# A hybrid decoder block: the first MLP group by plain products with a down product of its own, block sums built behind it, and down products that start with the last 256 tokens

## The chip, the cores and the metric

The kernel runs on one core of a Trainium2 chip. Five engines work side by side, each through its own instructions in order: PE (TensorE, matmuls), DVE (VectorE), ACT (ScalarE), POOL (GpSimd) and SP (SyncE, here the queue that issues nearly all loads). They wait for each other only where one needs what another has made. The metric is the device time of one execution in microseconds (us), and the time of a kernel is the median of its runs.

## The reference, cut to what matters

The block mixes 16 + 512 tokens (a delta-net branch and a sparse attention branch, merged and projected) and then applies an MLP with squared ReLU. The change touches the MLP alone; `h` has 512 rows that count and 1024 columns, `w_up` is 1024 x 4096 and `w_down` 4096 x 1024.

```
h = h + _rmsnorm(mix, post_mix_norm)
n2 = _rmsnorm(h, pre_mlp_norm)
u = jnp.square(jax.nn.relu(jnp.einsum('btd,df->btf', n2, w_up)))
h = h + _rmsnorm(jnp.einsum('btf,fd->btd', u, w_down), post_mlp_norm)
```

## The kernel before, in words

Every float32 operand of a matmul is split into a rounded part `hi` (ACT copies it) and a rest `lo` (DVE subtracts), and a product is three matmuls: hi x hi, hi x lo, lo x hi. The norm in front of the MLP is not applied to its operand: the row factor is taken out (squared ReLU is homogeneous), `mlp_scale` computes it, and only `down_last` uses it.

**Operands of the MLP.** The transposed tokens form a 2 x 2 matrix of blocks: rows are the two halves of the 1024 columns of `h`, columns the first 256 tokens (token tiles 0 and 1) and the second 256 (tiles 2 and 3). They are B11, B21 (first tokens), B12, B22 (second tokens). `mix_more(t)` transposes token tile t on PE (`n2t`), scales it into `fblock` (tile `F`) and lets `operand` make hi and lo.

**Up products.** `w_up` is taken in 8 groups of 512 columns; a group's weights are a 2 x 2 matrix of blocks too (A11, A12, A21, A22, each 128 x 1024 as laid out). `up(g)` multiplies the two matrices by Winograd's form of Strassen's scheme: seven products instead of eight, each of 24 matmuls of 128x256 (`product`). The scheme needs sums of blocks: of the weights (S1 to S4, in the tile `Ssum`, made per group by DVE) and of the tokens (T1 to T4, made once). `hidden(g, i, j, ..)` adds what belongs together, applies the squared ReLU and writes hi and lo of `u` for column half i and token half j.

**Down products.** `down(gs)` multiplies `u` of one or two groups by `w_down`: for each half of the 1024 output columns four PSUM tiles `d`, one for each token tile, gather over the chunks of weights (`proj_half`, whose matmuls are the lines 502 to 504 of `rows_part`), and `evac` copies (first time) or adds (later) them into `macc`. `down_last` does it for the last group.

**The order.** Groups 0 and 1 start interleaved, since only B11 and B21 exist while token tiles 2 and 3 are still being finished: the products A11 x B11 and A12 x B21 of both groups first (matmuls into X and Z of each), then the token sums T1 to T4, then the five others of group 0, of group 1, then `down((0, 1))` with four chunks for each half. From group 2 on it is `up(g)`, `down((g,))`, seven products and 96 matmuls of 128x512. The weights of groups 2 to 7 are loaded into the tile `R`, which lies in the slot `s6` and so wait until `u` of group 1, which lies there, has been used by its down product. A scheduler places instructions of the program on each engine by priority, so neighbouring steps mix.

Names in the rows: `d302` is `d` of group 3, column half 0, token tile 2. Views without such numbers write `d`. `hi_d`, `lo_d`, `side_pair` and `lo_side` hold weights; `raw_d` and `raw_up` are loads before they are split.

Of the kernel before, what the change touches and what calls it, by code (L numbers as in the profile page):

```python
# [10 lines left out]
F32 = mybir.dt.float32  # L11
# [3 lines left out]
ALU = mybir.AluOpType  # L15
# [23 lines left out]
def hybrid_block(ctx: ExitStack, tc: tile.TileContext, io: dict):  # L39
# [463 lines left out]
                TE.matmul(pt, lh, wlo, start=False, stop=False)  # L503
                TE.matmul(pt, ll, whi, start=False, stop=end)  # L504

    def proj_half(src, name, lhs, evac, chunks=4, room=lambda: None):

        pts = [stile(f"{name}{t}") for t in range(4)]
        for c in range(chunks):
            w = wload(src[c], 1024, f"{name}{c}", room())  # L510
            for t in range(NT):
                rows_part(pts[t], [(c, w)], lhs, t, slice(0, 512), c == 0, c == chunks - 1)
        for t in range(NT):
            evac(pts[t], t)

    def proj_rows(src, name, lhs, evac, done, more, room):
# [530 lines left out]


    bop = {x: mp.tile([P, 2, 4, 256], F32R, name=f"bop{x}") for x in ("B11", "B21", "B22", "T1")}
    late = {}  # L1050
    F = [cst.tile([P, 1024], F32, tag="st", name=f"F0{x}", bufs=2) for x in range(2)] + [wk.tile([P, 1024], F32, tag="tb", name=f"F1{x}", bufs=2) for x in range(2)]

    def fblock(b, t):

        return F[2 * b + t // 2][:, 512 * (t % 2) : 512 * (t % 2) + 512].rearrange("p (k t) -> p k t", t=P)

    def operand(x, t, src):
        nonlocal last_n2
        o = (bop[x] if x in bop else late[x])[:, :, :, t % 2 * P : t % 2 * P + P]
        S.copy(o[:, 0], src)  # L1060
        last_n2 = V.tensor_tensor(o[:, 1], src, f(o[:, 0]), ALU.subtract)

    def mix_more(t):

        for b in range(2):
            ps = stile(f"n2t{t}{b}")
            for k in range(4):
                kk = 4 * b + k
                TE.transpose(ps[:, k * P : (k + 1) * P], h2[:, t, kk * P : (kk + 1) * P], ident)
            gm = gmT[:, 4 * b : 4 * b + 4].rearrange("p (k o) -> p k o", o=1).to_broadcast([P, 4, P])  # L1070
            V.tensor_tensor(fblock(b, t), ps.rearrange("p (k t) -> p k t", t=P), gm, ALU.mult)
            if t < 2 or b:
                operand(f"B{b + 1}{t // 2 + 1}", t, fblock(b, t))
        if t > 1:
            b11, b21, b12, b22 = (fblock(b, u) for u in (t - 2, t) for b in range(2))
            V.tensor_tensor(b11, b12, b11, ALU.subtract)
            operand("T1", t, b11)
            V.tensor_tensor(b12, b22, b12, ALU.subtract)
            V.tensor_tensor(b22, b22, b11, ALU.subtract)
            V.tensor_tensor(b21, b21, b22, ALU.subtract)  # L1080

    def late_operands():
        t23 = slots.tile([P, 2, 2, 4, 256], F32R, tag="s1", name="t23")
        late["T2"], late["T3"] = t23[:, 0], t23[:, 1]
        for t in (2, 3):
            operand("T2", t, fblock(1, t))
        for t in (2, 3):
            operand("T3", t, fblock(0, t))
        t4 = [cst.tile([P, 1024], F32R, tag="st", name=f"t4{x}", bufs=2) for x in range(2)]
        for t in (0, 1):  # L1090
            o = [x.rearrange("p (k t) -> p k t", t=256)[:, :, t * P : t * P + P] for x in t4]
            S.copy(o[0], fblock(1, t))
            V.tensor_tensor(o[1], fblock(1, t), f(o[0]), ALU.subtract)
        late["T4"] = t4

    def mlp_scale(t):
        s1 = wk.tile([P, 1], F32, tag="s1", name=f"s1{t}", bufs=2)
        S.activation(gx[:, 1, :], h2[:, t, :], AF.Square, accum_out=s1)
        rms(rmlp[:, t : t + 1], s1, t, 1.0 / D, f"n2{t}")
        V.tensor_tensor(rmlp[:, t : t + 1], rmlp[:, t : t + 1], rmlp[:, t : t + 1], ALU.mult)  # L1100
        V.tensor_scalar(rmd[:, t : t + 1], rmlp[:, t : t + 1], rmlp[:, t : t + 1], 1.0 / D, ALU.mult, ALU.mult)

    def o_evac(pt, t, c0, n, i):
        cs = slice(c0, c0 + n)
# [23 lines left out]
    def pair(name):  # L1128

        nonlocal turn  # L1130
        turn += 1
        x = turn % (4 if "pair" in side else 3)
        if x == 3:
            return side["pair"]
        hi = wp.tile([P, 1024], F32R, tag="hl", name=f"hi_{name}", bufs=5)
        return [hi, side["lo"] if x == 2 else wp.tile([P, 1024], F32R, tag="hl", name=f"lo_{name}", bufs=5)]

    def up_block(i, k, g):

# [23 lines left out]
    def hidden(g, i, j, a, b=None):  # L1163
# [8 lines left out]
        o = us[g][:, :, 2 * i : 2 * i + 2, 256 * j : 256 * j + 256]  # L1172
        split(o[:, 0], o[:, 1], u.rearrange("p (a t) -> p a t", t=256))

    def up(g):

        first = g < 2
        nm = f"up{g}"
        if first:
            early = quarters_of(slots.tile([P, 4, 1024], F32R, tag="s2", name="eroom")) if g == 0 else None  # L1180
            rooms = [early[0:2], early[2:4]] if g == 0 else [[wp.tile([P, 1024], F32R, tag="hl", name=f"hl{g}{i}{x}", bufs=5) for x in range(2)] for i in range(2)]
            ws = []
            for k in range(2):
                raw = wp.tile([P, 1024], F32, tag="raw", name=f"raw_{nm}{k}", bufs=2)
                load(raw, 0, k, g)
                ws.append(parts(raw, rooms[k]))
            Z = ptile(f"{nm}Z")
            X = ptile(f"{nm}X", sp if g else pp)
            yield
            product(X, ws[0], bop["B11"], True)  # L1190
            E1 = copied(X, "cb", f"E1{g}")
            product(Z, ws[1], bop["B21"], True)
            yield
            us[g] = slots.tile([P, 2, 4, L], F32R, tag=("s2", "s6")[g], name=f"u{g}")
            hidden(g, 0, 0, E1, Z)
            yield
            R = {"21": gx[:, 2, :], "22": gx[:, 3, :]}
            for x in ("11", "12"):
                R[x] = wp.tile([P, 1024], F32, tag="raw", name=f"raw_{nm}{x}", bufs=2)
        else:  # L1200
            R = {x: side["R"][:, i, :] for i, x in enumerate(("11", "12", "21", "22"))}
        if "S" not in side:
            side["S"] = wk.tile([P, 1024], F32, tag="tb", name="Ssum", bufs=2)
            side["lo"] = wk.tile([P, 1024], F32R, tag="tb", name="lo_side", bufs=2)
        s_ = side["S"]
        for x in ("11", "21", "22", "12") if not first else ("21", "22", "11", "12"):
            load(R[x], int(x[0]) - 1, int(x[1]) - 1, g)
        if not first:
            X = ptile(f"{nm}X")
            product(X, parts(R["11"], pair(f"{nm}A11")), bop["B11"], True)  # L1210
            E1 = copied(X, "cb", f"E1{g}")
            us[g] = slots.tile([P, 2, 4, L], F32R, tag="s2", name=f"u{g}")
        V.tensor_tensor(s_, R["21"], R["22"], ALU.add)
        Y = ptile(f"{nm}Y")
        product(Y, parts(s_, pair(f"{nm}S1")), bop["T1"], True)
        E5 = copied(Y, "ca", f"E5{g}")
        V.tensor_tensor(s_, s_, R["11"], ALU.subtract)
        product(X, parts(s_, pair(f"{nm}S2")), late["T2"], False)
        U = copied(X, "cv", f"U{g}")
        V.tensor_tensor(s_, R["12"], s_, ALU.subtract)  # L1220
        product(Y, parts(s_, pair(f"{nm}S4")), bop["B22"], False)
        hidden(g, 0, 1, U, Y)
        V.tensor_tensor(R["21"], R["11"], R["21"], ALU.subtract)
        product(X, parts(R["21"], pair(f"{nm}S3")), late["T3"], False)
        hidden(g, 1, 1, E5, X)
        if not first:
            Z = ptile(f"{nm}Z")
            product(Z, parts(R["12"], pair(f"{nm}A12")), bop["B21"], True)
            hidden(g, 0, 0, E1, Z)
        product(X, parts(R["22"], pair(f"{nm}A22")), late["T4"], False)  # L1230
        hidden(g, 1, 0, X)

    def lhs(gs):
# [4 lines left out]
    def down(gs):  # L1238
# [9 lines left out]
        for hf in range(2):  # L1248
            c0 = 2 * (gs[0] % 2)
            n = 2 * len(gs)  # L1250
            proj_half(io["w_down"][g // 2][hf][c0 : c0 + n], f"d{g}{hf}", lhs(gs), lambda pt, t: evac(pt, t, hf), n, lambda: pair("d"))

    def down_last(g):

# [28 lines left out]
                d_evac(pt, t, cuts[i], n, i, end and i == 2)  # L1283
            out(t, len(cuts) - 1)

    ups = [up(g) for g in range(2)]
    for _ in range(3):
        for u in ups:
            next(u)
    late_operands()  # L1290
    with tc.issue_after(last_n2.ins):
        for t in range(NT):
            mlp_scale(t)
    for u in ups:
        for _ in u:
            pass
    down((0, 1))
    side["pair"] = quarters_of(slots.tile([P, 4, 1024], F32R, tag="s5", name="side_pair"))[0:2]
    turn = 3
    side["R"] = slots.tile([P, 4, 1024], F32, tag="s6", name="R")  # L1300
    for g in range(2, NG):
        for _ in up(g):
            pass
        if g < NG - 1:
            down((g,))
        else:
            down_last(g)
# [68 lines left out]
```

## Time and profile before

| | |
|---|---|
| median of 3 runs | 1092.55 us (1090.36 to 1095.31) |
| the profiled execution | 1095.43 us |
| its span in the profile | 1093.5 us |
| PE, DVE, ACT busy | 95%, 72%, 44% of the span |
| mean granted clock of PE | 0.978 of full speed |

The span runs from the first to the last instruction; 1.9 us of the execution lie around it. The granted clock is 1.00 at 2.4 GHz and 0.50 at 1.2 GHz, so a row between them mixes both. Starts are microseconds from the beginning of the span. The MLP of this profile runs from about 691 us to the end.

### The profile page before, as it was taken

The page shows a single profiled execution, that of the slowest core. Times are in us where ns is not written, and L with a number is a line of the kernel's source. Part 1 is how long each engine was busy: PE and PEld are TensorE (multiplying, and loading weights), DVE is VectorE, ACT ScalarE, POOL GpSimd, SP SyncE. Part 2 cuts the span into 40 slices and gives each one's busy share as a digit, 9 for nine tenths or more (in the row PEclk, how much of TensorE's full clock was granted, in tenths as well). Part 3 has the DMA queues.
Part 4 walks back from the last instruction along what each step waited for, and adds up shares of the span by engine and source line. Part 5 has one row for each costly group of instructions (what it writes and reads, how often), then busy time and mean ns, then how long its engine had stood idle before and what let it go on. Part 6 is the DMA issues. An engine that isn't in the chain of part 4 may idle for free.

```text
span 1093.5 us, 16951 instructions
## 1 busy us (share of the span) xinstructions
PE 1034.0 (95%) x6717; PEld 919.9 (84%) x6717; DVE 784.4 (72%) x1596; ACT 482.4 (44%) x852; POOL 62.2 (6%) x85
## 2 busy tenths in 40 slices
PE   7999999999999999999999999869978999999995
PEld 6999999989987888988888888768867978889794
DVE  5797898427599999668775546997146667576677
ACT  5555565444367522347655223454233324233241
POOL 4202303000000000000000000000000000000003
PEclk9999999999999999999999999989988999999997
DMA  5433425110132222231112363222333223133112
GB/s 174 124 110 88 127 79 147 44 39 21 59 100 76 70 86 97 97 97 58 59 39 78 97 221 107 77 78 97 97 116 116 82 92 117 59 115 97 58 39 78
DMA packets 33424, 98.61 MB, mean 90 GB/s; under 512 B 3696, under 2 KB 4032, under 8 KB 33344
## 3 DMA queue, kind: packets, MB, share of 16 engines
q1 hardware_dynamic: 30624, 89.60, 25.8%
q0 software_dynamic: 2720, 7.92, 3.1%
q8 instruction: 53, 0.87, 0.3%
q14 instruction: 27, 0.22, 0.1%
HBM read 92.23 MB, written 5.28 MB: 89 GB/s over the span
## 4 chain that ended last, share of the span: by engine, by line
PE 78%; DVE 13%; DMA 3%; ACT 3%; issue 2%; SPq 0%; DVEq 0%; ACTq 0%
PE d L502 5%; PE d L503 5%; PE d L504 5%; PE pa_dense L886 2%; PE pa_dense L885 2%; PE pa_dense L884 2%; PE pb_z L543 1%; PE pa_q L192 1%; PE pa_q L194 1%; PE pa_bg L192 1%; PE pa_q L193 1%; PE pa_bg L193 1%; PE bd L1006 1%; PE bd L1007 1%; PE bd L1005 1%
## 5 line engine op out<-in xcount | busy, mean ns | idle before, releaser
L502 PE MATMUL d<-hi_d,u 128*128 128x512 f32 (+1 forms) x212 | 84.1, 397 | 5.5 <-ACT u L700 5.5
L504 PE MATMUL d<-hi_d,u 128*128 128x512 f32 (+1 forms) x212 | 82.9, 393 | 0.0
L503 PE MATMUL d<-lo_d,u 128*128 128x512 f32 (+1 forms) x140 | 54.9, 392 | 0.0
L502 PEld LDWEIGHTS d<-hi_d,u 128*128 128x128 f32 x212 | 40.3, 190 | 15.1 <-ACT u L700 6.1
L504 PEld LDWEIGHTS d<-hi_d,u 128*128 128x128 f32 x212 | 40.1, 189 | 9.4
L884 PE MATMUL pa_dense<-nhi,hi_dense 128*128 128x512 f32 x96 | 39.3, 409 | 0.0
L97 ACT CAST hi_d<-raw_d 128x1024 fp32r<-128x1024 f32 x26 | 27.3, 1050 | 25.3 <-PE d L503 12.7
L886 PE MATMUL pa_dense<-nhi,lo_dense 128*128 128x512 f32 x96 | 38.1, 397 | 0.0
L885 PE MATMUL pa_dense<-nlo,hi_dense 128*128 128x512 f32 x96 | 38.0, 396 | 0.0
L543 PE MATMUL pb_z<-hi_z,nhi 128*128 128x256 f32 x128 | 37.6, 294 | 0.0
L192 PE MATMUL pa_k<-nhi,hi_k 128*128 128x264 f32 x128 | 37.1, 290 | 0.0
L192 PE MATMUL pa_v<-nhi,hi_v 128*128 128x264 f32 x128 | 37.0, 289 | 0.0
L192 PE MATMUL pa_q<-nhi,hi_q 128*128 128x258 f32 x128 | 36.8, 287 | 0.0
L194 PE MATMUL pa_k<-nhi,lo_k 128*128 128x264 f32 x128 | 36.7, 288 | 0.0
L544 PE MATMUL pb_z<-lo_z,nhi 128*128 128x256 f32 x128 | 36.6, 286 | 0.0
L545 PE MATMUL pb_z<-hi_z,nlo 128*128 128x256 f32 x128 | 36.4, 285 | 0.0
L194 PE MATMUL pa_v<-nhi,lo_v 128*128 128x264 f32 x128 | 36.4, 284 | 0.0
L193 PE MATMUL pa_v<-nlo,hi_v 128*128 128x264 f32 x128 | 36.4, 284 | 0.0
L193 PE MATMUL pa_k<-nlo,hi_k 128*128 128x264 f32 x128 | 36.3, 284 | 0.0
L194 PE MATMUL pa_q<-nhi,lo_q 128*128 128x258 f32 x128 | 36.1, 282 | 0.0
L193 PE MATMUL pa_q<-nlo,hi_q 128*128 128x258 f32 x128 | 36.0, 281 | 0.0
L700 ACT CAST u<-u 128x512 fp32r<-128x512 f32 x32 | 19.7, 619 | 28.1 <-DVE u L1171 22.5
(875 smaller groups left out, 3459.5 us busy)
## 6 DMA issues: line engine op xcount, KB each, us to landing
raw_d<-w_down SPq DMA_DIRECT2D x32, 512.0 KB, 3.6
R<-w_up SPq DMA_DIRECT2D x24, 512.0 KB, 3.9
raw_k<-w_k SPq DMA_DIRECT2D x8, 512.0 KB, 4.0
raw_v<-w_v SPq DMA_DIRECT2D x8, 512.0 KB, 4.5
raw_q<-w_q SPq DMA_DIRECT2D x8, 512.0 KB, 3.5
raw_z<-w_z SPq DMA_DIRECT2D x8, 512.0 KB, 3.7
raw_w_ga<-w_ga SPq DMA_DIRECT2D x8, 512.0 KB, 3.6
raw_bg<-w_bg SPq DMA_DIRECT2D x8, 512.0 KB, 3.6
```

What stands on the lines that cost most here:

```text
L192: TE.matmul(pt[:m, :n], hi[:, ws], mh[:, k, ms], start=(k == 0), stop=False)
L193: TE.matmul(pt[:m, :n], hi[:, ws], ml[:, k, ms], start=False, stop=False)
L194: mark = TE.matmul(pt[:m, :n], lo[:, ws], mh[:, k, ms], start=False, stop=(k == KT - 1))
L502: TE.matmul(pt, lh, whi, start=beg, stop=False)
L503: TE.matmul(pt, lh, wlo, start=False, stop=False)
L504: TE.matmul(pt, ll, whi, start=False, stop=end)
L543: TE.matmul(pt, nhi[:, k, ts], whi, start=(k == 0), stop=False)
L544: TE.matmul(pt, nhi[:, k, ts], wlo, start=False, stop=False)
L545: mm = TE.matmul(pt, nlo[:, k, ts], whi, start=False, stop=(k == KT - 1))
L884: TE.matmul(pt, hi[:, ws], nhi[:, k, NM:], start=(k == 0), stop=False)
L885: TE.matmul(pt, hi[:, ws], nlo[:, k, NM:], start=False, stop=False)
L886: mm = TE.matmul(pt, lo[:, ws], nhi[:, k, NM:], start=False, stop=(k == KT - 1))
```

## The change

It replaces the interleaved start of groups 0 and 1. Group 0 is now done by `up_plain`: eight plain products (192 matmuls of 128x256, in four PSUM tiles of 48), whose operands are B11, B21, B12, B22 and weights without sums. Then come the token sums, `down((0,))` alone, `mlp_scale` for all four token tiles at once, `up(1)` by the seven products, `down((1,))`, and the rest as before. B12 is a new operand; T3 later takes its place in the same tile. `u` of group 0 lies in slot `s6`, that of group 1 in `s2`. Every `down` now takes the token tiles in the order 2, 3, 0, 1.

```
-    def proj_half(src, name, lhs, evac, chunks=4, room=lambda: None):
+    def proj_half(src, name, lhs, evac, chunks=4, room=lambda: None, order=range(NT)):
...
-            for t in range(NT):
+            for t in order:
                 rows_part(pts[t], [(c, w)], lhs, t, slice(0, 512), c == 0, c == chunks - 1)
-        for t in range(NT):
+        for t in order:
             evac(pts[t], t)
...
-            if t < 2 or b:
-                operand(f"B{b + 1}{t // 2 + 1}", t, fblock(b, t))
-        if t > 1:
+            operand(f"B{b + 1}{t // 2 + 1}", t, fblock(b, t))
+
+    def token_sums():
+        for t in (2, 3):
             b11, b21, b12, b22 = (fblock(b, u) for u in (t - 2, t) for b in range(2))
             V.tensor_tensor(b11, b12, b11, ALU.subtract)
             operand("T1", t, b11)
...
+    def mlp_scale():
+        sm = wk.tile([P, NT], F32, tag="s1", name="s1n", bufs=2)
+        for t in range(NT):
+            S.activation(gx[:, 1, :], h2[:, t, :], AF.Square, accum_out=sm[:, t : t + 1])
+        V.tensor_scalar(sm, sm, 1.0 / D, EPS, ALU.mult, ALU.add)
+        rsqrt(rmlp, sm, (P, NT), "n2")
...
+    def up_plain(g):
+
+        early = quarters_of(slots.tile([P, 4, 1024], F32R, tag="s2", name="eroom"))
+        ws = [wload(io["w_up"][4 * g + m], 1024, f"up{g}{m}", (early[0:2], early[2:4], None, None)[m]) for m in range(4)]
+        us[g] = slots.tile([P, 2, 4, L], F32R, tag="s6", name=f"u{g}")
+        for j in range(2):
+            for i in range(2):
+                pt = ptile(f"up{g}{i}{j}")
+                for m in range(2):
+                    hi, lo = ws[2 * i + m]
+                    o = pt[:, 256 * m : 256 * m + 256]
+                    for k in range(KT):
+                        b = bop[f"B{k // 4 + 1}{j + 1}"]
+                        ks = slice(k * P, (k + 1) * P)
+                        for n, (x, y) in enumerate(((hi, 0), (hi, 1), (lo, 0))):
+                            TE.matmul(o, x[:, ks], b[:, y, k % 4, :], start=m + k + n == 0, stop=m == 1 and k == KT - 1 and n == 2, skip_group_check=True)
+                hidden(g, i, j, pt)
...
-            proj_half(io["w_down"][g // 2][hf][c0 : c0 + n], f"d{g}{hf}", lhs(gs), lambda pt, t: evac(pt, t, hf), n, lambda: pair("d"))
+            proj_half(io["w_down"][g // 2][hf][c0 : c0 + n], f"d{g}{hf}", lhs(gs), lambda pt, t: evac(pt, t, hf), n, lambda: pair("d"), (2, 3, 0, 1))
...
-    ups = [up(g) for g in range(2)]
...
-    down((0, 1))
+    up_plain(0)
+    token_sums()
+    down((0,))
+    mlp_scale()
+    up(1)
+    down((1,))
```

The first place is PE's order behind the transposes of token tile 3 (`n2t30`, `n2t31`). Before, one product of group 1 follows, and then the first product that needs a weight sum and T1 (`up0Y`):

```order
L1069 MATMUL n2t30_7129<-ident_78,h2_6714 128x128 x4
L1069 MATMUL n2t31_7135<-ident_78,h2_6714 128x128 x4
L1156 MATMUL up1X_7180<-bopB11_6724,hl100_7167 128x256 x2
L1156 MATMUL up1X_7180<-bopB11_6724,hl101_7168 128x256
L1156 MATMUL up0Y_7389<-bopT1_6727,hi_up0S1_7390 128x256 x2
L1156 MATMUL up0Y_7389<-bopT1_6727,lo_up0S1_7391 128x256
```

Now the second tokens' plain products follow (B12 is the first half of the tile `b12t2`), 96 matmuls in two PSUM tiles, and then the down product of group 0:

```order
L1072 MATMUL n2t30_7126<-ident_78,h2_6714 128x128 x4
L1072 MATMUL n2t31_7134<-ident_78,h2_6714 128x128 x4
L1191 MATMUL up001_7279<-b12t2_7115,eroom_7149 128x256
L1191 MATMUL up011_7333<-b12t2_7115,hi_up02_7160 128x256
L1191 MATMUL up001_7279<-b12t2_7115,eroom_7149 128x256 x11
L1191 MATMUL up001_7279<-bopB22_6726,eroom_7149 128x256 x12
L1191 MATMUL up011_7333<-b12t2_7115,hi_up02_7160 128x256
L1191 MATMUL up011_7333<-b12t2_7115,lo_up02_7161 128x256
L502 MATMUL d002_7415<-hi_d_7417,u0_7170 128x512
L503 MATMUL d002_7415<-lo_d_7418,u0_7170 128x512
```

Between the transposes and the first matmul on a block sum there were 24 matmuls; there are now 96 of them and the 96 matmuls of a down product.

The second place is SP's queue ahead of group 2. Before, the loads of group 2's weights (`R`) stand behind all loads of the double down product:

```order
L93 DMA raw_d112_7910<-w_down 128x1024
L93 DMA raw_d113_7940<-w_down 128x1024
L93 DMA raw_d200_8208<-w_down 128x1024
L93 DMA raw_d201_8238<-w_down 128x1024
L1143 DMA R_7973<-w_up 128x2x512 x8
L93 DMA raw_d210_8276<-w_down 128x1024
```

Now they stand behind the first load of group 1's down product, ahead of its three others:

```order
L1144 DMA raw_up111_7572<-w_up 128x2x512
L1144 DMA raw_up112_7573<-w_up 128x2x512
L93 DMA raw_d100_7813<-w_down 128x1024
L1144 DMA R_7943<-w_up 128x2x512 x4
L93 DMA raw_d101_7843<-w_down 128x1024
L93 DMA raw_d110_7880<-w_down 128x1024
```

What they wait for is the slot `s6`: it was the end of `down((0, 1))` and is now the end of `down((0,))`.

The third place is PE's first down matmuls of group 3 (groups 4 to 6 read alike). Before:

```order
L1156 MATMUL up3X_8341<-t40_7302,lo_up3A22_8534 128x256
L502 MATMUL d300_8566<-hi_d_8570,u3_8370 128x512
L503 MATMUL d300_8566<-lo_side_7383,u3_8370 128x512
L502 MATMUL d301_8567<-hi_d_8570,u3_8370 128x512
L503 MATMUL d301_8567<-lo_side_7383,u3_8370 128x512
L502 MATMUL d302_8568<-hi_d_8570,u3_8370 128x512
```

Now:

```order
L1157 MATMUL up3X_8311<-t40_7407,lo_up3A22_8504 128x256
L502 MATMUL d302_8538<-hi_d_8540,u3_8340 128x512
L503 MATMUL d302_8538<-lo_side_7575,u3_8340 128x512
L504 MATMUL d302_8538<-hi_d_8540,u3_8340 128x512
L502 MATMUL d303_8539<-hi_d_8540,u3_8340 128x512
L503 MATMUL d303_8539<-lo_side_7575,u3_8340 128x512
L502 MATMUL d300_8536<-hi_d_8540,u3_8340 128x512
```

Twelve matmuls on token tiles 2 and 3 now stand ahead of the first on tile 0.

## Rows read from the trace of the kernel before

**Rows 1.** The page's busy shares.

```profile
PE 1034.0 (95%) x6717; PEld 919.9 (84%) x6717; DVE 784.4 (72%) x1596; ACT 482.4 (44%) x852; POOL 62.2 (6%) x85
```

**Rows 2.** What PE waited for from 690 us to the end: us in total, times, longest (eleven rows, 33.9 us together; the five smallest, 2.7 us, are left out).

```profile
PE d L502 <- ACT u L700: 10.6, 5, 3.3
PE up0Y L1156 <- ACT hi_up0S L700: 9.1, 1, 9.1
PE up2X L1156 <- ACT hi_up2A L700: 5.1, 1, 5.1
PE up1Y L1156 <- DVE lo_up1S L701: 2.6, 1, 2.6
PE up1Z L1156 <- DVE hl L701: 2.1, 1, 2.1
PE n2t L1069 <- DVE h L1042: 1.7, 2, 1.4
...
```

**Rows 3.** Stretches of the MLP: length, busy us and count for PE, PEld, DVE, ACT, POOL, then the granted clock, the DMA share and GB/s.

```profile
691.30:709.30 18.00, 14.24 (x113) 13.22 (x111) 18.00 (x40) 7.17 (x12) 0.00 (x0) 1.00 0.39 117
718.50:724.50 6.00, 5.34 (x26) 5.05 (x27) 5.89 (x18) 1.04 (x1) 0.00 (x0) 0.57 0.28 87
740.30:744.50 4.20, 4.20 (x22) 4.20 (x23) 3.06 (x4) 1.04 (x1) 0.00 (x0) 0.59 0.30 91
806.50:813.00 6.50, 5.99 (x28) 5.70 (x29) 5.67 (x5) 1.26 (x2) 0.00 (x0) 0.54 0.37 136
833.80:840.00 6.20, 6.16 (x15) 4.86 (x16) 3.56 (x4) 0.51 (x1) 0.00 (x0) 0.52 0.55 172
...
969.00:971.00 2.00, 1.55 (x4) 1.26 (x5) 2.00 (x3) 1.92 (x3) 0.00 (x0) 0.62 0.79 207
```

**Rows 4.** The time line of PE: the first up matmuls, the transposes of token tile 3 and the product behind them, the first down matmul of group 2 at the full clock and, 72 down matmuls later, the first matmul of group 3. Columns: start, length, instruction, count, idle time before it and what ended that.

```profile
691.32 1.76 PE L1156 MATMUL up0X<-bopB,eroom 128*128 128x256 f32 x13
...
705.23 1.29 PE L1069 MATMUL n2t<-ident,h 128*128 128x128 f32 x8 [1.37 <-DVE h L1042]
706.28 3.06 PE L1156 MATMUL up1X<-bopB,hl 128*128 128x256 f32 x24
...
842.19 0.40 PE L502 MATMUL d<-hi_d,u 128*128 128x512 f32 x1
...
859.01 1.23 PE L1156 MATMUL up3X<-bopB,side_pair 128*128 128x256 f32 x9
```

And one product of 24 matmuls from the chain that ended last: start, length, count.

```profile
750.82 2.82 PE up1X L1156 x24
```

**Rows 5.** The time line of DVE between token tile 3 (`h`) and the first weight sum. Same columns.

```profile
704.34 1.41 DVE L1042 SCALAR_TENSOR_TENSOR h<-h,r,xs 128x512 f32<-128x512 f32 x2
...
706.26 1.28 DVE L1071 TENSOR_TENSOR F<-n2t,gmT 128x512 f32<-128x512 f32 x2
...
709.87 0.68 DVE L1078 TENSOR_TENSOR F<-F,F 128x512 f32<-128x512 f32 x1
...
716.14 1.21 DVE L1213 TENSOR_TENSOR Ssum<-gx 128x1024 f32<-128x1024 f32 x1
...
718.66 1.22 DVE L701 TENSOR_TENSOR lo_up0S<-Ssum,hi_up0S 128x1024 fp32r<-128x1024 f32 x1
```

**Rows 6.** The time line of ACT in the same stretch.

```profile
710.59 0.62 ACT L1060 CAST t<-F 128x512 fp32r<-128x512 f32 x1 [0.63 <-DVE F L1078]
...
717.39 1.04 ACT L700 CAST hi_up0S<-Ssum 128x1024 fp32r<-128x1024 f32 x1 [0.19 <-DVE Ssum L1213]
```

**Rows 7.** Loads: what SP's queue waited for between 640 and 840 us (this row of it is the load of `R`), the first uses of `R` on ACT and DVE, the time from issue to landing of the 8 loads of `R` between 640 and 840 us, and the page's row on the 32 loads of `raw_d` (KB each, median us to landing).

```profile
SPq L1143 <- PE d L504: 14.3, 1, 14.3
...
805.45 1.04 ACT L700 CAST hi_up2A<-R 128x1024 fp32r<-128x1024 f32 x1 [3.39 <-DMA R<-w_up]
...
808.41 1.23 DVE L1213 TENSOR_TENSOR Ssum<-R 128x1024 f32<-128x1024 f32 x1 [0.66 <-DMA R<-w_up]
...
DMA to landing us min/median/max: 3.6/4.5/6.7
...
raw_d<-w_down SPq DMA_DIRECT2D x32, 512.0 KB, 3.6
```

**Rows 8.** Groups 3 to 6: the first matmul of groups 4, 5, 6 and 7; what PE waited for from 859 us on; the first down matmul of group 5; in group 3, DVE writing the rest of `u` for the second tokens and ACT writing `u` for the first tokens.

```profile
903.25 0.40 PE L1156 MATMUL up4X<-bopB,hi_up4A 128*128 128x256 f32 x2
...
947.53 0.40 PE L1156 MATMUL up5X<-bopB,hi_up5A 128*128 128x256 f32 x2
...
993.38 0.40 PE L1156 MATMUL up6X<-bopB,hi_up6A 128*128 128x256 f32 x2
...
1037.62 2.55 PE L1156 MATMUL up7X<-bopB,side_pair 128*128 128x256 f32 x20
...
PE d L502 <- ACT u L700: 7.3, 4, 1.9
...
969.45 0.80 PE L502 MATMUL d<-hi_d,u 128*128 128x512 f32 x1 [1.85 <-ACT u L700]
...
877.14 0.68 DVE L701 TENSOR_TENSOR u<-u,u 128x512 fp32r<-128x512 f32 x1
...
880.18 0.62 ACT L700 CAST u<-u 128x512 fp32r<-128x512 f32 x1 [0.50 <-DVE u L1171]
```

**Rows 9.** The adding `evac` of a down product: shortest, median and longest ns.

```profile
L1246 DVE TENSOR_TENSOR macca<-macca,d x20: 678/680/690, 844.6 to 1035.9; 128x512 f32<-128x512 f32 x20
```

More of the change, by code (lines that the diff above doesn't have):

```diff
@@ L1049, in hybrid_block @@
     bop = {x: mp.tile([P, 2, 4, 256], F32R, name=f"bop{x}") for x in ("B11", "B21", "B22", "T1")}
-    late = {}
     F = [cst.tile([P, 1024], F32, tag="st", name=f"F0{x}", bufs=2) for x in range(2)] + [wk.tile([P, 1024], F32, tag="tb", name=f"F1{x}", bufs=2) for x in range(2)]
@@ L1055, in fblock, with operand @@
         return F[2 * b + t // 2][:, 512 * (t % 2) : 512 * (t % 2) + 512].rearrange("p (k t) -> p k t", t=P)
-    def operand(x, t, src):
+    def operand(x, t_, src):
         nonlocal last_n2
-        o = (bop[x] if x in bop else late[x])[:, :, :, t % 2 * P : t % 2 * P + P]
+        if x == "B12" and x not in bop:
+            t = slots.tile([P, 2, 2, 4, 256], F32R, tag="s1", name="b12t2")
+            bop["B12"] = bop["T3"] = t[:, 0]
+            bop["T2"] = t[:, 1]
+        o = bop[x][:, :, :, t_ % 2 * P : t_ % 2 * P + P]
         S.copy(o[:, 0], src)
@@ L1079, in mix_more @@
             V.tensor_tensor(b22, b22, b11, ALU.subtract)
+            operand("T2", t, b22)
             V.tensor_tensor(b21, b21, b22, ALU.subtract)
[L1082 to L1086, printed above, removed]
         for t in (2, 3):
@@ L1093, in late_operands @@
             V.tensor_tensor(o[1], fblock(1, t), f(o[0]), ALU.subtract)
[L1094 to L1101, printed above, removed]
+        bop["T4"] = t4
+    def mlp_scale():
[4 more added lines that the diff above has]
+        rsqrt(rmlp, sm, (P, NT), "n2")
+        V.tensor_tensor(rmlp, rmlp, rmlp, ALU.mult)
+        V.scalar_tensor_tensor(rmd, rmlp, 1.0 / D, rmlp, ALU.mult, ALU.mult)
     def o_evac(pt, t, c0, n, i):
@@ L1135, in pair @@
         hi = wp.tile([P, 1024], F32R, tag="hl", name=f"hi_{name}", bufs=5)
-        return [hi, side["lo"] if x == 2 else wp.tile([P, 1024], F32R, tag="hl", name=f"lo_{name}", bufs=5)]
+        return [hi, side["lo"] if x == 2 and "lo" in side else wp.tile([P, 1024], F32R, tag="hl", name=f"lo_{name}", bufs=5)]
     def up_block(i, k, g):
@@ L1173, in hidden @@
         split(o[:, 0], o[:, 1], u.rearrange("p (a t) -> p a t", t=256))
+    def up_plain(g):
[14 more added lines that the diff above has]
+                hidden(g, i, j, pt)
     def up(g):
-        first = g < 2
         nm = f"up{g}"
[L1179 to L1196, printed above, removed]
+        if g == 1:
             R = {"21": gx[:, 2, :], "22": gx[:, 3, :]}
@@ L1205, in up @@
         s_ = side["S"]
-        for x in ("11", "21", "22", "12") if not first else ("21", "22", "11", "12"):
+        for x in ("11", "21", "22", "12"):
             load(R[x], int(x[0]) - 1, int(x[1]) - 1, g)
[L1208 to L1212, printed above, removed]
+        X = ptile(f"{nm}X")
+        product(X, parts(R["11"], pair(f"{nm}A11")), bop["B11"], True)
+        E1 = copied(X, "cb", f"E1{g}")
+        us[g] = slots.tile([P, 2, 4, L], F32R, tag="s2", name=f"u{g}")
         V.tensor_tensor(s_, R["21"], R["22"], ALU.add)
@@ L1217, in up @@
         V.tensor_tensor(s_, s_, R["11"], ALU.subtract)
-        product(X, parts(s_, pair(f"{nm}S2")), late["T2"], False)
+        product(X, parts(s_, pair(f"{nm}S2")), bop["T2"], False)
         U = copied(X, "cv", f"U{g}")
@@ L1223, in up @@
         V.tensor_tensor(R["21"], R["11"], R["21"], ALU.subtract)
-        product(X, parts(R["21"], pair(f"{nm}S3")), late["T3"], False)
+        product(X, parts(R["21"], pair(f"{nm}S3")), bop["T3"], False)
         hidden(g, 1, 1, E5, X)
[L1226 to L1230, printed above, removed]
+        Z = ptile(f"{nm}Z")
+        product(Z, parts(R["12"], pair(f"{nm}A12")), bop["B21"], True)
+        hidden(g, 0, 0, E1, Z)
+        product(X, parts(R["22"], pair(f"{nm}A22")), bop["T4"], False)
         hidden(g, 1, 0, X)
@@ L1284, in down_last @@
             out(t, len(cuts) - 1)
-    ups = [up(g) for g in range(2)]
[L1287 to L1296, printed above, removed]
-    down((0, 1))
+    up_plain(0)
[4 more added lines that the diff above has]
+    down((1,))
     side["pair"] = quarters_of(slots.tile([P, 4, 1024], F32R, tag="s5", name="side_pair"))[0:2]
@@ L1301, in hybrid_block @@
     for g in range(2, NG):
-        for _ in up(g):
-            pass
+        up(g)
         if g < NG - 1:
```

## Prediction

> **What bounds the kernel now.** I read the busy shares first: PE is busy for 95% of the span, 1034.0 of 1093.5 us [rows 1], so that idle PE alone could give at most 59 us. But a busy PE counts matmuls at both clock levels alike, so the next views are the waits of PE in the MLP, where the change lies, and the granted clock of its stretches. PE waits for 33.9 us there. The reader is to see who ends these waits: the first product on a weight sum (`up0Y`) waits 9.1 us, the first of group 2 (`up2X`) 5.1, `up1Y` 2.6, `up1Z` 2.1, the transposes of token tiles 2 and 3 together 1.7, and the first matmul of five down products 10.6 [rows 2]. Four of these waits are followed by stretches in which the clock is granted at 0.57, 0.59, 0.54 and 0.52, so mostly at 1.2 GHz [rows 3].
>
> Behind the first group of waits stands DVE, busy for 18.00 of 18.00 us from 691.3 us on [rows 3]: token tile 3, its block sums, T2 to T4 and only then the first weight sum, which it reaches at 716.14, with its lo part done at 719.9 [rows 5]. Behind `up2X` stands a load: `R` waits 14.3 us in SP's queue for the slot that the double down product still reads, and ACT then 3.39 us for its landing [rows 7]. The stretch that counts for groups 0 to 2 runs from the first up matmul, 691.32, to the first of group 3, 859.01 [rows 4]: 167.7 us.
>
> **What that stretch is made of.** A product of 24 matmuls takes 2.82 us, and 72 down matmuls take 859.01 - 842.19 = 16.82, so 0.2336 each; eight transposes take 706.28 - 705.23 = 1.05 [rows 4]. 21 products make 59.2, 288 down matmuls 67.3, 16 transposes 2.1: 128.6 us of work. Idle: 33.9 less the 7.3 that lie behind 859 us [rows 2, 8], so 26.6. Lost to the clock, length times what was not granted: 6.0 x 0.43 + 4.2 x 0.41 + 6.5 x 0.46 + 6.2 x 0.48 = 10.3 [rows 3]. The sum is 165.5; 2.2 remain as gaps, which I keep on both sides. So 36.9 us are waits and their clock.
>
> **The change, part by part.** *Plain products in group 0* add one product: +2.8 us of PE. They need no weight sums, so that DVE drops four sums of 1.2 us and three splits of as much for that group, and three of four chains of `mlp_scale`.
>
> *Behind token tile 3.* The first 48 matmuls are as many as X and Z of group 0 were, and the next 48 end at 691.32 + 96 x 0.1175 + 8 transposes + 0.3 of wait for tile 2 (1.7 less 1.37), about 704. DVE's queue up to `h` of tile 3 is about as long as before (its first half lands at about 705 [rows 5]), so PE waits 1.0 there; I keep the 0.3. The transposes end at 706.2, and DVE scales them into `F` from 706.26, for 1.28 us [rows 5]. Now B12 is late next: ACT has a square of 1 us ahead of its hi cast (a 128x512 cast is 0.62 [rows 6]), DVE a rest of `u` ahead of its lo (steps of 0.6), so hi stands at 707.5 and lo at 708.5; PE waits 2.1 more. Together 3.4 us of idle. These short pauses lie close together, as the pause of 2.6 at 740 does, behind which the clock was 0.59 for 4.2 us [rows 2, 3]; the pauses of 2.1 and 1.4 around 701 and 704 cost nothing, 1.00 from 691.3 to 709.3 [rows 3]. The bounds are 0 and 3.0 us; the nearest row is that of 740, so I take 1.7. The Trainium skill speaks against the change here: "TensorE: Matmul & The Clock Gate", section "A second HAM failure mode: psum-queue depth-cycling", says that frequent short pauses between groups of matmuls make the clock swing between its levels. By it the 1.7 would be paid, without it not; this trace agrees at 740 us and not before 709 us.
>
> *The cover.* From 708.5 the second tokens' products run for 94 x 0.1175, to 719.5, and `down((0,))` for 96 x 0.2336 = 22.4, to 742. T1 to T4, `mlp_scale` and the first weight sums of group 1 lie beside that and cost PE nothing, if two waits hold. First, the second chunk of d002 needs the last `u`: relu, square, hi and lo behind 719.5. ACT has the cast of `raw_d010` ahead of that hi, and that load is issued when DVE has split `raw_d000` (718.6), landing 3.6 later [rows 7]; cast at 723.4, hi at 724.0, lo at 724.7. PE arrives at 719.5 + 24 x 0.2336 = 725.1: a margin of 0.4, and each us beyond it is one of PE. Second, DVE makes group 2's first weight sum ahead of `lo_up1S3`, so that it stands still until `R` has landed, and behind it wait the splits of S3, A12 and A22 and the first `u` of group 1. `R` is issued at 742 and its third load landed 6.9 after the slot came free (801.5 to 808.4 [rows 7]): 749, the sum at 750.2, the split at 751.4; PE wants it after four products, at 753.3. Margin 1.9. On ACT, `raw_d000` (landing near 702.8) is waited for ahead of T2 and the relu of `u`; tile 3 comes later than that, so nothing is added.
>
> *The load of `R`*, with the slot free at 742 and group 2 starting at 742 + 19.7 + 22.4 = 784, has 35 us to land: the 5.1 us and their clock go. *Two more evacuations* of 4 x 0.68 us on DVE [rows 9] lie beside down matmuls, as in every later group.
>
> *Order 2, 3, 0, 1.* In group 3 the rest of `u` for the second tokens is written from 877.14, while PE waited for the first tokens' cast of 880.18 [rows 8]. Twelve matmuls on tiles 2 and 3 are 2.8 us of work, more than the 1.9 that the longest of the four waits took [rows 8]. So the four waits of groups 3 to 6 go, 7.3 us, and group 2's 3.3 with its clock. Group 5 took 993.38 - 947.53 = 45.85 where group 4 took 44.28 [rows 8]: behind its wait of 1.85 the clock was 0.62 [rows 3, 8]. That 1.6 goes too: 8.9 for groups 3 to 6.
>
> **The sum.** Stretch to group 3: -36.9 + 2.8 + 3.4 + 1.7 = -29.0. Groups 3 to 6: -8.9. Together -37.9. The profiled execution, 1095.43 us with 1.9 us around its span, would take 1057.5. The median is 2.9 below that execution, so I forecast 1092.55 - 37.9 = 1054.6 us.
>
> **Rivals.** *DVE stays the bound.* For: it was never idle from 691 to 709 us [rows 3], and the margin at d002 is 0.4. Against: its load falls by some 15 us while PE's cover grows. If it falls back as before, the waits on `up0Y` and `up1Y` return at a later place: 9.1 + 2.6 and 4.3 of clock, 16.0, so 1070.6. Falling 3 us behind and paying the clock once gives 1060.
>
> *The new order removes no wait.* Then a split of `w_down` or the second tokens' `u` would be what PE really waited for. Against: both are written before PE is free [rows 8]. Price: 8.9, and group 2's 3.3 with 3.0 of clock, 15.2: 1069.8.
>
> *Slower, by the clock.* If the pauses at 705 to 708 us left PE at 1.2 GHz for long, each us of work at that level would cost half a us. To eat 37.9 it would have to last 76 us, and 87 us for 0.5% slower (1098): all of the plain products, both down products and `up(1)`. Against: the longest such stretch here is 6.5 us [rows 3].
>
> *Nothing happens*: several of these together, near 1090.
>
> **Chances and range.** Forecast 0.73, with its own range 1049 (no new pause, no clock lost: -43.0) to 1063 (a margin missed by 3 us with its clock, half of the 7.3 kept). DVE 0.13, order 0.07, clock 0.04, nothing 0.03. The range 1047 to 1068 reaches 2 us below the sum without pauses, for the gaps, and towards the two rivals at 1070. A difference of 0.5% (5.5 us) is about what a measurement tells from none: faster 0.93, same 0.03, slower 0.04.
>
> **What would show it.** In the profile after, `up0Y` is gone and no wait of several us stands on PE between 709 and 790 us; pauses of about 1 and 2 us stand behind token tile 3, with a low clock behind them or not; `up2X` starts near 784 without waiting for a load; group 3 starts near 830 where it was 859; groups 4 to 7 follow each other by 42.4 us, with no wait on the first down matmul. I am wrong if d002 or `up1X` waits for DVE for more than 2 us, if `R` lands after 751 and `up1X` stands still, or if the down products now wait on tile 0 twelve matmuls later.

## The result, and the profile after

The changed kernel takes 1056.4 us (median; 1055.23 to 1056.86), beside 1092.53 us for the kernel before on the same chip: ratio 0.9666, 95% interval 0.9643 to 0.969. The forecast was 1054.6 with its own range 1049 to 1063, so direction and size were right. One step of the working was right in its number and wrong in its reason, and the experiments show which.

The page of the changed kernel: busy shares, against [rows 1].

```profile
PE 1025.7 (97%) x6741; PEld 914.7 (87%) x6741; DVE 777.7 (74%) x1563; ACT 480.2 (46%) x851; POOL 62.8 (6%) x85
```

24 matmuls more, and yet PE is busy for 8.3 us less: a matmul in a stretch of low clock counts with its longer time (15 down matmuls fill the 6.2 us at 0.52 in [rows 3], 0.41 each, where 72 of them take 16.82 us at the full clock, 0.23 each), and fewer such stretches are left. What PE waited for from 690 us to the end (us in total, times, longest; all six rows), against [rows 2]:

```profile
PE up L1191 <- ACT b12t L1063: 1.5, 1, 1.5
PE d L504 <- DVE u L701: 0.5, 1, 0.5
PE n2t L1072 <- DVE h L1042: 0.4, 2, 0.3
PE d L502 <- ACT u L700: 0.3, 1, 0.3
PE up L1191 <- DVE b12t L1064: 0.3, 1, 0.3
PE up L1191 <- DVE lo_up L98: 0.3, 1, 0.3
```

33.9 us of waits have become 3.3; `up0Y`, `up2X`, `up1Y`, `up1Z` and the five waits of the down products are gone but for 0.3. The granted clock behind token tile 3 (stretch, busy us and count of PE, PEld, DVE, ACT, POOL, then the clock), against [rows 3]:

```profile
704.00:709.00 5.00, 3.27 (x23) 2.44 (x22) 4.96 (x10) 4.46 (x8) 0.00 (x0) 1.00 0.11 43
709.00:714.00 5.00, 4.76 (x27) 4.76 (x28) 5.00 (x12) 1.67 (x3) 0.00 (x0) 0.66 0.00 0
714.00:1000.00 286.00, 285.19 (x1754) 253.73 (x1754) 198.40 (x237) 110.96 (x138) 0.00 (x0) 1.00 0.32 100
```

Up to 1000 us one stretch of 5 us is left at 0.66; 5.00 x 0.34 = 1.7 us lost, where the forecast put 1.7. The time line of PE, at the places of [rows 4] and [rows 8] (start, length, instruction, count, idle time before it and what ended it):

```profile
691.97 1.75 PE L1191 MATMUL up<-bopB,eroom 128*128 128x256 f32 x13
...
705.67 1.29 PE L1072 MATMUL n2t<-ident,h 128*128 128x128 f32 x8 [0.16 <-DVE h L1042]
708.45 0.39 PE L1191 MATMUL up<-b12t,eroom 128*128 128x256 f32 x1 [1.49 <-ACT b12t L1063]
...
709.24 1.76 PE L1191 MATMUL up<-b12t,eroom 128*128 128x256 f32 x11 [0.28 <-DVE b12t L1064]
...
786.61 0.41 PE L1157 MATMUL up2X<-bopB,hi_up2A 128*128 128x256 f32 x2
...
829.18 3.04 PE L1157 MATMUL up3X<-bopB,side_pair 128*128 128x256 f32 x24
...
999.42 3.04 PE L1157 MATMUL up7X<-bopB,side_pair 128*128 128x256 f32 x24
```

Groups 0 to 2 take 829.18 - 691.97 = 137.2 us (before 167.7, forecast 138.7). Groups 3 to 6 take 999.42 - 829.18 = 170.2 (before 1037.62 - 859.01 = 178.6, forecast 8.9 less, measured 8.4 less).

The point at which the MLP starts differs from kernel to kernel: its first matmul stands between 689.6 and 692.0 us in the ten profiles, though the change lies behind it. So below, stretches are compared from the first up matmul of each kernel; a median has that scatter in it. And a profile shows one execution: that of the kernel before took 1095.43 us, 2.9 more than the median, so that a difference between two profiles and one between two medians can be some us apart.

### The profile page after: what moved, and what is told of

Same layout as the page of the kernel before. It is cut to its first block, busy times and chain, and to the rows that moved or that the text cites. A ratio compares the mean times of both kernels' runs of the same rounds, so it can differ in the third digit from the quotient of the medians.

```text
span 1055.0 us, 16952 instructions
## 1 busy us (share of the span) xinstructions
PE 1025.7 (97%) x6741; PEld 914.7 (87%) x6741; DVE 777.7 (74%) x1563; ACT 480.2 (46%) x851; POOL 62.8 (6%) x85
## 4 chain that ended last, share of the span: by engine, by line
PE 85%; DVE 9%; ACT 2%; DMA 2%; issue 1%; SPq 0%; DVEq 0%; ACTq 0%
PE d L504 5%; PE d L502 5%; PE d L503 5%; PE pa_dense L885 2%; PE pa_dense L886 2%; PE pa_dense L884 2%; PE pa_q L192 1%; PE pa_q L194 1%; PE pa_bg L192 1%; PE pa_q L193 1%; PE pa_bg L193 1%; PE bd L1006 1%; PE bd L1005 1%; PE bd L1007 1%; PE pa_bg L194 1%; PE pb_z L543 1%
## 5 line engine op out<-in xcount | busy, mean ns | idle before, releaser
L503 PE MATMUL d<-lo_d,u 128*128 128x512 f32 (+1 forms) x156 | 60.6, 389 | 0.0
L503 PEld LDWEIGHTS d<-lo_d,u 128*128 128x128 f32 x156 | 29.3, 188 | 6.7
```

## The experiments

All are timed in three to five rounds against the kernel before, which was at 1093.75 us in the first four and at 1093.33 in the others; ratios are against it. "Stretch" is groups 0 to 2, from the first up matmul to the first matmul of `up3X`.

| kernel | median us | ratio, 95% interval | stretch us | groups 3 to 6 us |
|---|---|---|---|---|
| before | 1092.53 | 1 | 167.7 | 178.6 |
| changed | 1056.4 | 0.9666 (0.9643 to 0.969) | 137.2 | 170.2 |
| changed, first tokens first in the down products | 1065.59 | 0.9747 (0.9731 to 0.9763) | 139.5 | 178.2 |
| changed, `R` made late | 1065.52 | 0.9742 (0.9727 to 0.9757) | 147.2 | 169.9 |
| changed, one joint down product | 1058.33 | 0.9678 (0.9664 to 0.9693) | 140.4 | 169.8 |
| changed, group 0 by seven products | 1068.73 | 0.9764 (0.9742 to 0.9786) | 149.8 | 169.0 |
| changed, token sums later | 1051.87 | 0.9612 (0.9592 to 0.9632) | 133.1 | 170.1 |
| before with the new order | 1080.05 | 0.988 (0.9865 to 0.9895) | 162.4 | 169.0 |
| before with the slots swapped | 1082.15 | 0.9893 (0.9871 to 0.9916) | 154.4 | 177.1 |
| before with both | 1070.61 | 0.9786 (0.9766 to 0.9806) | 152.7 | 169.0 |

### The order of the token tiles, undone and alone

The changed kernel without the new order:

```diff
-            proj_half(..., lambda: pair("d"), (2, 3, 0, 1))
+            proj_half(..., lambda: pair("d"))
```

> The changed kernel with the down products of groups 0 to 6 taking the token tiles in the order 0, 1, 2, 3 again; nothing else is undone. Theory (the new order removes the waits for the first tokens' u): in groups 3 to 6 the four waits of 1.8 us on the first down matmul come back with a low clock behind some, 8.4 us (what groups 3 to 6 became shorter by), and groups 1 and 2 get a wait of 1.8 each: 12 us more than the changed kernel, 1068. Rival (the order changes nothing, the periods shrank for another reason): 1056.

Measured 1065.59. The waits of PE from 690 us on, largest row, and the first two of the five places on the time line:

```profile
PE d L502 <- ACT u L700: 10.3, 5, 2.6
```

```profile
805.56 0.50 PE L502 MATMUL d<-side_pair,u 128*128 128x512 f32 x1 [1.80 <-ACT u L700]
...
851.41 0.50 PE L502 MATMUL d<-hi_d,u 128*128 128x512 f32 x1 [1.81 <-ACT u L700]
```

All five waits are back, in groups 2 to 6; `down((0,))` and `down((1,))` have none, though one was expected in group 1 too. Groups 3 to 6 are 7.9 us longer than in the changed kernel. Group 2, from `up2X` to `up3X`, takes 829.55 - 783.32 = 46.2 us where it takes 42.6 in the changed kernel: 3.7 more, its wait and a clock of 0.68 from 805 to 810 us. Together 11.6 us, where 12 were expected. By the ratios it is 8.9: in this profile the first two groups were 1.4 us shorter (93.3 against 94.6; two matmuls of the down product fill a part of the pause behind token tile 3) and the MLP began 1.9 us earlier.

The new order put alone into the kernel before:

> The kernel before with the token order 2, 3, 0, 1 in its down products and nothing else of the change. Theory: the five waits on the first down matmul go, 10.6 us, with the low clock behind two of them, 3.0 and 1.6: 15.2 us less than before, 1077. If only the waits go and the clock stays as it was, 1082. Rival (the order is worth something only together with the other parts): 1092.

Measured 1080.05, 13.1 us by the ratio, where 15.2 were expected; by the profiles it is 5.3 in the stretch and 9.6 in groups 3 to 6, 14.9. The first matmuls of the down products wait 0.7 us in all, the other waits of [rows 2] stand:

```profile
PE up0Y L1156 <- ACT hi_up0S L700: 9.1, 1, 9.1
PE up2X L1156 <- ACT hi_up2A L700: 5.1, 1, 5.1
PE up1Y L1156 <- DVE lo_up1S L701: 2.8, 1, 2.8
...
PE d L502 <- ACT u L700: 0.7, 1, 0.7
```

So the order removes four of the five waits that it was said to remove, and 2.6 of the 3.3 us of the fifth, that of group 2. Its 3.0 us of clock go along: that stretch of [rows 3], 833.8 to 840.0 at 0.52, is at 1.00 here.

```profile
833.00:840.00 7.00, 6.73 (x29) 5.50 (x30) 5.98 (x7) 1.79 (x3) 0.00 (x0) 1.00 0.44 146
```

### The load of R

In the changed kernel `u` of group 1 is put into slot `s6` too, so that `R` has to wait for the end of `down((1,))`:

```diff
-        us[g] = slots.tile([P, 2, 4, L], F32R, tag="s2", name=f"u{g}")
+        us[g] = slots.tile([P, 2, 4, L], F32R, tag="s6" if g == 1 else "s2", name=f"u{g}")
```

> The changed kernel with u of group 1 in the slot s6 too, behind u of group 0, so that the loads of R for group 2 wait for the end of group 1's down product as they did before; everything else stays. Theory (the wait on R at group 2 was worth its own 5.1 us and the clock behind it, 3.0): up2X waits 5 us for R's landing, the clock falls, 1064.5. Rival (before, that wait hid other lateness of group 2, so that undoing it costs more: the weight sums of group 2 pile up behind R): 1068 or more. Rival (the load was hidden anyway): 1056.

Measured 1065.52: by the ratios 8.3 us more than the changed kernel, against 8.1 expected, and 10.0 by the stretch. The wait of PE and the clock behind it:

```profile
PE up2X L1157 <- ACT hi_up2A L700: 5.4, 1, 5.4
```

```profile
791.00:798.00 7.00, 6.41 (x28) 6.12 (x29) 6.06 (x5) 1.64 (x4) 0.00 (x0) 0.50 0.31 115
```

The wait has its old size, and behind it lie 7 us at 0.50, the lower of the two levels: 3.5 us lost, where the theory had 3.0. Of the first rival's pile-up behind `R` there are waits of 0.5 and 0.6 us in group 2. Whether the load is early is worth this much.

### One joint down product

If `down((0,))` is what covers DVE's work on the token sums and releases the slot of `R`, then a joint down product behind both groups must bring both waits back:

```diff
-    down((0,))
     mlp_scale()
     up(1)
-    down((1,))
+    down((0, 1))
```

> The changed kernel with group 0's plain products kept, but its down product joined with that of group 1 again behind up(1), so that no down product lies between the plain products and the first product on a weight sum. R waits for the end of the joint down product, as in e3. Theory (the down product of group 0 covers the sums): besides e3's 8 us, PE waits on DVE and ACT for T3, T4 and the first weight sums of group 1, 4 to 8 us, and pays a low clock of 2 to 3 us behind it: 1070 to 1075. Rival (the plain products alone gave DVE enough time): as e3, 1064.5.

Both missed. Measured 1058.33, 1.3 us above the changed kernel by the ratios, whose intervals overlap, and 3.2 by the stretch. The waits of PE from 690 us on, the four largest:

```profile
PE up1Y L1157 <- DVE lo_side L701: 1.6, 1, 1.6
PE up L1191 <- ACT b12t L1063: 1.5, 1, 1.5
PE up1Y L1157 <- DVE lo_up1S L701: 0.5, 1, 0.5
PE up1X L1157 <- DVE lo_up1S L701: 0.5, 1, 0.5
```

DVE comes too late by 1.6 us and two times 0.5 and no more: the plain products of group 0 alone give it nearly all the time that it needs. And `R` isn't late at all: it is wanted at 788.07, the first matmul of `up2X` in this kernel, and on SP's time line its loads are issued from 777.06 us on, before the joint down product ends (the line merges the four loads for group 2, issued in 1.9 us, with the four for group 3):

```profile
777.06 22.39 SPq L1144 DMA_DIRECT2D R<-w_up  x8
```

The reason is a part of the change that I had not priced by itself. In the kernel before `u` of group 0 lies in `s2` and `u` of group 1 in `s6`; now they lie the other way round. A joint down product reads group 0 in the first two of its four chunks and group 1 in the last two, once for each half of the output columns, so with group 0 in `s6` that slot comes free after six of eight chunks and not at the end.

### The slots alone

The kernel before with only that swap, and with the swap and the new order:

```diff
-            us[g] = slots.tile([P, 2, 4, L], F32R, tag=("s2", "s6")[g], name=f"u{g}")
+            us[g] = slots.tile([P, 2, 4, L], F32R, tag=("s6", "s2")[g], name=f"u{g}")
```

> The kernel before with one edit: the slots of u0 and u1 change places (u0 in s6, u1 in s2), so that R, which comes into s6, has to wait only for the last read of u0, three quarters through the joint down product, and not for its end. Theory (what moved R's load in the changed kernel is this swap and not the split of the down product): the wait of 5.1 us at the head of group 2 goes, with some 3 us of clock behind it: 1084.5 us. Rival: the load is late for another reason, or u0, which must now wait in s6 until the last token tile's residual has been read, holds the vector engine earlier: 1092 us or more.

Measured 1082.15, 11.7 us by the ratio, where 8 were expected. `up2X` waits for nothing, and `R` is issued at 789.75 where before it was 801.47:

```profile
789.75 1.92 SPq L1143 DMA_DIRECT2D R<-w_up  x4
```

The gain is more than that because group 2's down product gains as well: its wait, 3.3 us in [rows 2], is 1.44 here, and the stretch of 0.52 behind it is at 1.00. This profile is of the shortest of the kernel's four executions (1079.89 us; the others took 1082.02 to 1082.85), so how much of that clock the others kept isn't shown.

```profile
822.54 0.50 PE L502 MATMUL d<-side_pair,u 128*128 128x512 f32 x1 [1.44 <-ACT u L700]
```

```profile
822.00:829.00 7.00, 6.46 (x28) 5.33 (x29) 5.14 (x6) 2.73 (x4) 0.00 (x0) 1.00 0.61 194
```

> The kernel before with two edits: the slot swap of u0 and u1, and the down products' order 2, 3, 0, 1; both groups still by seven products, one joint down product. If the two act in different places their gains add: 13.1 us measured for the order alone and 8 expected for the swap give 1071.5 us, and what is left to the changed kernel, 15 us, is the plain products of group 0 and the later sums. Rival: both remove part of the same idle time, for instance because the load of R, which now starts earlier, only uncovers another wait at the head of group 2: 1077 us or more.

Measured 1070.61, near the 1071.5 of adding gains, 23.4 us by the ratio: the parts, 13.1 and 11.7, add up within their intervals. By the stretches they overlap, 5.3 and 13.3 against 15.0, and both do take the same 3.0 us of clock in group 2, and parts of the same wait. What is left on PE is above all the wait for the sums (the two largest rows):

```profile
PE up0Y L1156 <- ACT hi_up0S L700: 9.1, 1, 9.1
PE up1Y L1156 <- DVE lo_up1S L701: 2.8, 1, 2.8
```

From here to the changed kernel it is 0.0120 of 1093 us, so 13 us: the plain products, the sums behind them and the split of the down product.

### Group 0 by seven products

The changed kernel with its plain products taken back (`up(0)` loads its blocks as `up(1)` does, and `u` of group 0 stays in `s6`):

```diff
...
-    up_plain(0)
     token_sums()
+    up(0)
     down((0,))
```

> The changed kernel with group 0 by the seven products again (token sums first, since they need them), everything else as changed: its own down product, order 2, 3, 0, 1, u0 in s6. Theory (the plain products are what fills the time in which the vector engine makes the token sums): only A11 by B11, 2.8 us, can run before the sums; the residual of the last token tile was there at 705.6 us and the first sums some 5 us later, so TensorE is idle for about 14 us, with 4 us of clock, less 2.8 us for the product saved: 1072 us. Rival: without the plain group's weight splits the vector engine gets to the last token tile by 700 us and to the first sum by 703 us; 8 us idle, less 2.8: 1062 us.

Measured 1068.73, 10.7 us above the changed kernel by the ratios, between the two numbers. The waits of PE:

```profile
PE up0Y L1157 <- ACT hi_up0S L700: 9.7, 1, 9.7
PE n2t L1072 <- DVE h L1042: 6.9, 2, 6.7
```

The residual of token tile 3 comes early (the transposes at 700.71, as the rival had it), but then PE waits 9.7 us for the first product on a sum, far longer than the rival had it: on DVE the sums T1 to T4 of the last tiles stand ahead of the weight sum. The idle time grows by 14.6 us (0.24, 6.65, 9.71 and 0.53 against 2.5), about what the theory had, and the product saved takes 2.8 back. The clock is at its lower level from the transposes to about 717 us:

```profile
710.00:715.00 5.00, 2.11 (x8) 1.81 (x9) 4.96 (x9) 1.12 (x2) 0.00 (x0) 0.50 0.00 0
715.00:720.00 5.00, 5.00 (x35) 5.00 (x35) 3.66 (x11) 2.75 (x4) 0.00 (x0) 0.76 0.38 108
```

Half of 2.11 and 5.00 x 0.24 are 2.3 us lost, and the eight transposes take 1.94 instead of 1.29: 2.9, so 1.2 more than the 1.7 of the changed kernel, where the theory had 4. That makes 13.0, against the 12.6 us by which the stretch is longer; groups 3 to 6 are 1.2 us shorter. So of the last 13 us the plain products bring most, and the split of the down product 1 to 3. No run has the seven products with the weight sum ahead of T1 to T4 on DVE, so how much of the 9.7 us another order there would save stays open.

### The pause at token tile 3

What is left of idle time in groups 0 to 2 of the changed kernel, 2.5 us, stands around token tile 3 for the most part. On DVE (time line of the changed kernel) the sums of tiles 0 and 2 run between the steps of tile 3's scale, so that its residual `h` begins only at 704.77:

```profile
702.53 0.69 DVE L1082 TENSOR_TENSOR F<-F,F 128x512 f32<-128x512 f32 x1
...
703.26 0.69 DVE L1083 TENSOR_TENSOR F<-F,F 128x512 f32<-128x512 f32 x1
...
703.98 0.69 DVE L1085 TENSOR_TENSOR F<-F,F 128x512 f32<-128x512 f32 x1
...
704.77 1.42 DVE L1042 SCALAR_TENSOR_TENSOR h<-h,r,xs 128x512 f32<-128x512 f32 x2
```

Nothing needs these sums before group 1. So they are held back, with the squares of `mlp_scale`, until the operands of tile 3 are made:

```diff
-    token_sums()
+    with tc.issue_after(last_n2.ins):
+        token_sums()
     down((0,))
-    mlp_scale()
+    with tc.issue_after(last_n2.ins):
+        mlp_scale()
```

> The changed kernel with the token sums and the Squares of the tokens held back, on their engines, until the operands of the last token tile are made, so that the vector engine comes to that tile's scale and residual before the sums. Theory (the pause at token tile 3 is the vector engine's order, no lack of time): the transposes of that tile move in among the products of the first two token tiles, the idle 0.2, 1.5 and 0.3 us go and with them the 1.7 us of clock behind: 1052.7 us. Rival: the sums, done later, come in the way of the last block of u0, whose margin in the down product is 0.5 us, and of group 1's first weight sums: waits of 2 us or more there, no change or slower: 1056 to 1059 us.

Measured 1051.87, the fastest of all, where 1052.7 was expected: 0.9612 against 0.9666, 5.9 us with intervals that lie apart, and in the traces 781.51 - 690.97 = 90.5 us from the first up matmul to `up2X` where the changed kernel takes 94.6. Of the gain of 4.1, 2.0 is idle time (2.5 less the 0.4 that are left here, at tile 2 and a split) and 1.7 the clock; 0.4 I can't place. The transposes of tile 3 now stand among the products of the first tokens, four at 702.25 us and four at 702.91, and the two stretches that answer to those above are full:

```profile
702.25 0.63 PE L1072 MATMUL n2t<-ident,h 128*128 128x128 f32 x4
```

```profile
704.00:709.00 5.00, 5.00 (x44) 4.95 (x43) 4.45 (x8) 4.13 (x8) 0.00 (x0) 1.00 0.01 3
709.00:714.00 5.00, 5.00 (x45) 5.00 (x44) 4.97 (x10) 1.90 (x4) 0.00 (x0) 1.00 0.00 0
```

The rival's waits don't come: from 720 us to `up2X` PE waits for nothing.

## Why the prediction was right, and where it was not

**The account of the stretch** held. Work of 128.6 + 2.8, idle time of 2.5 and 1.7 of clock make 135.6 of the 137.2 measured, so 1.6 are gaps where I had kept 2.2.

**The pause behind token tile 3** was forecast as 0.3, 1.0 and 2.1, measured as 0.28 and 0.27 (tile 2, and a split), 0.16, 1.49 and 0.28: 2.5 against 3.4. The 1.0 failed, and the 2.1 came out as 1.8. For the 1.0 I had taken DVE's queue up to `h` to be about as long as before, and PE to get there at about 704. `h` began 0.4 later than before (704.77 against 704.34), but PE got there at 705.5 (705.67 less its wait): it had started 0.65 later, and waited 0.25 more on the way, and the products and transposes between took some 0.6 longer than my 0.1175 and 1.05 make.

**The clock.** The 1.7 was taken by the nearest row, between bounds of 0 and 3.0, and came out as 1.7; that the two are equal is luck. That it hangs on this pause the other kernels show. Without the pause it isn't lost (the token sums later), and with a pause of 0.83 instead of 1.49 in the kernel with the first tokens first it isn't either (first row). Where the pause is 1.49 again it is lost again, with `R` made late and with one joint down product (second and third row):

```profile
707.00:712.00 5.00, 4.72 (x40) 4.70 (x40) 5.00 (x12) 1.60 (x3) 0.00 (x0) 1.00 0.00 0
...
708.00:713.00 5.00, 4.82 (x27) 4.82 (x28) 5.00 (x12) 1.72 (x3) 0.00 (x0) 0.66 0.00 0
...
706.00:711.00 5.00, 4.37 (x21) 4.17 (x22) 5.00 (x11) 2.27 (x5) 0.00 (x0) 0.66 0.00 0
```

The Trainium skill, "TensorE: Matmul & The Clock Gate", section "A second HAM failure mode: psum-queue depth-cycling", says that frequent short pauses make the clock swing. By it the 1.7 was to be paid, and at 709 us the trace agrees. The five waits of 1.8 to 2.6 us in the kernel with the first tokens first stand some 45 us apart, so they don't test what it says of frequent ones; of them only the one in group 2 has a low clock behind it (0.68 from 805 to 810 us; 1.00 from 850 to 856, and so behind the other three):

```profile
805.00:810.00 5.00, 4.44 (x13) 3.53 (x14) 4.94 (x6) 2.08 (x3) 0.00 (x0) 0.68 0.58 197
...
850.00:856.00 6.00, 4.59 (x20) 3.75 (x21) 4.87 (x7) 2.43 (x4) 0.00 (x0) 1.00 0.43 131
```

So the size of one pause doesn't tell it.

**The cover** is the step that failed in its reason. No wait of several us stands between 709 and 790 us, as forecast, and both margins were met: the last `u` of group 0 (its rest) was written at 726.89 + 0.69 = 727.6 and first used at 728.08, a margin of 0.5 where I had 0.4, and the third load of `R` came in at 752.21:

```profile
726.89 0.69 DVE L701 TENSOR_TENSOR u<-u,u 128x512 fp32r<-128x512 f32 x1 [1.22 <-ACT u L700]
...
752.21 1.23 DVE L1212 TENSOR_TENSOR Ssum<-R 128x1024 f32<-128x1024 f32 x1 [1.86 <-DMA R<-w_up]
753.35 1.22 DVE L701 TENSOR_TENSOR lo_up1S<-gx,hi_up1S 128x1024 fp32r<-128x1024 f32 x1
```

The split that waits behind it was done at 754.6, and PE wanted it at 755.95, in the third matmul of that product: a margin of 1.4 where I had 1.9. All of it came 2.5 us later than I had it, with the first down matmul at 721.99 instead of 719.5; 1.7 of that is the clock, which the prediction charged in its sum but left out of these times.

```profile
721.99 0.40 PE L502 MATMUL d<-hi_d,u 128*128 128x512 f32 x1
...
755.95 0.28 PE L1157 MATMUL up1X<-b12t,lo_up1S 128*128 128x256 f32 x1
```

But I had credited the 22.4 us of `down((0,))` with covering the sums. The joint down product shows that they were hardly needed: the plain products cover the sums up to waits of 1.6, 0.5 and 0.5 us.

**The load of R.** The price, 5.1 and its clock, 8.1 together, is right: with `R` made late again 8.3 by the ratios, 10.0 by the stretch. The reason was half right: an early `R` comes from where `u` of group 0 lies; the down product of its own only makes it earlier still.

**The order** had 8.9 in groups 3 to 6 and 3.3 with 3.0 of clock in group 2, 15.2. Alone it gave 13.1 (14.9 by the profiles); in the changed kernel 11.6 by stretches, of which group 2 is 3.7: part of group 2's wait goes with the early `R` already (1.44 instead of 3.3 with the slots swapped alone). The gain of groups 3 to 6 fell short by 0.5. In group 4 a load of weights came late, the split and the last `u` wait behind it on ACT, and PE waits 0.29 and 0.49 us for that `u`; that group took 914.87 - 871.37 = 43.5 us instead of 42.2:

```profile
890.93 1.05 ACT L97 CAST side_pair<-raw_d 128x1024 fp32r<-128x1024 f32 x1 [1.81 <-DMA raw_d<-w_down]
```

**The rivals.** DVE did not stay the bound: PE waits for nothing between 709.24 and 894 us. The order did remove its waits, and the clock was low for 5 us, not 76.

## What to carry to other kernels

A wait that is removed is priced by its trace row, but who removes it has to be asked of every part of the change, the places of its buffers included: here a swap of two slots was worth 11.7 us by itself and would have been had without any new product. Where an engine falls behind at the seam between two phases, look at what stands in its queue ahead of the work that the next engine waits for, and hold back what is needed only later: 4 us more by the stretch came from the same work in another order.

## What the runs showed of the hardware that I had not expected

Two waits in a row shared their cost: with `R` early (the slots alone), the wait at the next down product, 22 us later, shrank from 3.3 to 1.44 us, and the 6.2 us at a clock of 0.52 behind it were at 1.00 in that profile. And pauses of like size differ in what follows: the clock fell behind 1.80 us at 805 us and not behind 1.81 at 851 us in one and the same kernel (changed, first tokens first). The pause at token tile 3 brought a low clock in each of the three kernels where it was 1.49 us, and none where it was 0.83.
